# Prompt attention in units of four query tiles, with the values as TensorE's weights in two column halves

## The chip, the cores and the metric

The kernel runs on one NeuronCore of one Trainium2 chip. The metric is the device time of one execution in microseconds (us). TensorE (PE) multiplies matrices: it loads a block of weights and streams another operand past it, into PSUM. VectorE (DVE), ScalarE (ACT) and GpSimd (POOL) work element by element, and SyncE (SP) issues the transfers between HBM and SBUF. Each engine takes its instructions in the order of its own list and waits on semaphores for the others.

## The reference

One decoder layer for two groups: a prompt of 1024 tokens and 8 sample requests of 4 tokens each with 4096 cached tokens in pages. The layer has a mixer (a gated MLP, and attention over latents with 8 heads), attention to a memory, and a gated FFN with a short convolution. The change lies in the mixer. Cut to its core:

```python
def chunk_gmlp(u, v, w_s, b_s, ln_g, ln_b):          # the gate of phase 1
    vg = layer_norm(gelu(v).reshape(n, t // c, c, A_GROUPS, A_GROUP_DIM), ln_g, ln_b)
    mixed = einsum('gts,nmsgd->nmtgd', tril(w_s), vg) + b_s...
    return gelu(u) * mixed.reshape(n, t, A_WIDTH)

q = qk_rope(rms_norm((rms_norm(cq) @ w_uq)...))      # 8 heads, 64 + 32 (rope)
k = qk_rope(rms_norm(concat([ckv_n @ w_uk, k_pe])))
v = ckv_n @ w_uv                                     # 8 heads x 64
s = einsum('...qhd,...khd->...hqk', q, k) * 96 ** -0.5
p = softmax(where(k_pos <= q_pos, s, NEG_INF))
b_out = einsum('...hqk,...khd->...qhd', p, v)
x = x + concat([rms_norm(a_out), rms_norm(b_out)]) @ w_o
```

All inputs and outputs are float32.

## The kernel before

The stages follow each other in the profiled execution: phase 1 with the projections and the gate (to about 208 us), prompt attention (to 427), the sample's paged attention (to 900), output projection and memory attention (to 1187), FFN (to the end). Helpers come back everywhere: `mm3` (L185) does a product of operands that are split into a high and a low part, as three matmuls; `split` writes the high part on ACT (L191 or L195) and the low part on DVE (L192 or L198); `rsqrt_steps` (L222 to L245) takes a root by two Newton steps, 11 DVE operations, or three on DVE and 13 on GpSimd where it is given that engine. Names in the rows are tiles: kTh and kTl are the two parts of the transposed keys of a head, qTh and qTl of its queries, s a bank of scores in PSUM, pr and prs probabilities, pth their transposed copy, o the output, wsum a block of FFN weights.

**Phase 1.** Tokens are in tiles of 128: eight of the prompt, and the ninth holds the sample's 32. `squares(c)` sums the squares of three tiles on ACT and takes their roots (rs_tok) on DVE. The gate runs in two halves of channels; for each group of tiles it takes gelu (ACT L457), a layer norm (DVE L458 to L472), a split (vgh, vgl) and the product with wsh, wsl on TensorE. The order of the four engines is what a scheduler made of the code in this phase.

**Prompt attention** (`phase2a`, L640). Its order is written out by hand, under `manual_schedule`. `proj_group` projects latents to q, k and v for half of the heads (hf) and tiles i0 to i1, and norms them (L855 to L876, rope on GpSimd, L602 to L605); `head_prep` transposes q and k of one head (L899) and splits them. `head_unit` gives the functions of one unit, which is one head and **two query tiles** (G = 0 to 3): scores with the row maximum (L923 to L932; keys in one chunk up to 512, else in two; the s banks are two), `expo` (L936), `trans` (transposes of the probabilities to keys by queries and a copy on ACT, L945 and L947), `value` (L957: pth, 128 keys by 128 queries, is the weight, and 64 columns of v stream by), and `out` (reciprocal of the sum, product into b_all or b_last). 32 units make 80 steps. A step transposes bank j of its unit, writes out what is done, does the exps that are pending, computes scores of the unit **two ahead**, and does the values of the step before. The lists `extra` put the other work into steps: head_prep of the next heads, projections of the second half of the heads, and from step 22 on, every four steps, `weight_sums`, which GpSimd forms for the FFN from 1 MB blocks (13 of them, four operations of 128x512 each, L794 to L797). Three of the four groups of two tiles are normed and transposed for the output projection (`mix_steps`, L1536 to L1552) in the last steps, one in the sample's attention. `sample()` starts the sample's preparation and its first page loads at step 41.

**Start of prompt attention.** Before the first unit, all of q and k of the first four heads is projected and normed, and head 0 is transposed whole. `proj_weights` loads and splits the second heads' weights at that place.

## Time and profile before

| | |
|---|---|
| median of three runs | 1867.06 us (1865.72 to 1868.98) |
| the profiled execution | 1869.48 us |
| its span, first to last instruction | 1867.6 us |
| busy: PE, PE's weight loads, DVE, ACT, POOL | 98%, 94%, 73%, 50%, 36% |
| mean granted clock of TensorE | 0.988 |

The busy shares are averages over stages. A row of a group shows line, engine, operation, output and inputs with their sizes, the count, the busy time and the mean ns of one; behind the second bar stands the idle time ahead of them and what ended it. Matmuls overlap, so that the mean of one is longer than the distance between two starts. The granted clock is 1.00 at full speed. In a row of the timeline the first number is the start in us, the second the time to the end of the group.

### The profile page before, as it was taken

How to read it: one execution, taken by the hardware profiler on the slowest of the kernel's cores; microseconds unless marked ns; L12 is line 12 of the kernel's file. 1: busy time of each engine (PE TensorE's matmuls, PEld its weight loads, DVE VectorE, ACT ScalarE, POOL GpSimd, SP SyncE). 2: the span in 40 equal slices, each digit the busy share in tenths (PEclk: the TensorE clock that was granted, in tenths of full speed). 3: DMA queues.
4: the chain of work that ended last, by engine and by line, in shares of the span. 5: the costliest groups of instructions: out<-in, count | busy, mean ns of one | idle time of the engine just before them, and what ended most of it. 6: DMA issues, size and time to landing. Idle time of an engine off the chain costs nothing.

```text
span 1867.6 us, 39666 instructions
## 1 busy us (share of the span) xinstructions
PE 1823.0 (98%) x14414; PEld 1754.7 (94%) x14414; DVE 1355.3 (73%) x2824; ACT 928.1 (50%) x1965; POOL 679.1 (36%) x784
## 2 busy tenths in 40 slices
PE   9999899989999999999999999999999999999999
PEld 8899899888999999998899988899999999999999
DVE  7864756655877767776744675888888888879664
ACT  7335776665555555555543455533323333344442
POOL 0011306643535445443313110267776677500000
PEclk9999899989999999999999999999999999999999
DMA  8102205556776666564554345412222222495252
GB/s 321 41 10 67 79 1 193 213 214 190 216 207 182 181 172 194 164 187 132 178 167 132 127 159 152 140 59 85 77 90 82 69 79 71 118 349 170 76 154 76
DMA packets 129414, 260.17 MB, mean 139 GB/s; under 512 B 20417, under 2 KB 70434, under 8 KB 126146
## 3 DMA queue, kind: packets, MB, share of 16 engines
q1 hardware_dynamic: 128354, 256.58, 43.7%
q8 instruction: 114, 1.87, 0.4%
q10 hardware_dynamic: 864, 1.05, 0.2%
q14 instruction: 82, 0.67, 0.1%
HBM read 212.27 MB, written 45.30 MB: 138 GB/s over the span
## 4 chain that ended last, share of the span: by engine, by line
PE 81%; issue 5%; DMA 4%; DVE 4%; SPq 3%; ACT 2%; POOL 2%; DVEq 0%; POOLq 0%; ACTq 0%
PE s L185 15%; PE d L185 12%; PE mm L185 9%; PE F L185 7%; PE b L185 7%; PE X L185 7%; PE E L185 7%; PE A L185 3%; PE o L957 3%; PE y L185 3%; PE tp L945 1%; SPq L1248 1%; DMA cT<-cT 1%; PE o L1395 1%; DMA ck<-ck 1%
## 5 line engine op out<-in xcount | busy, mean ns | idle before, releaser
L185 PE MATMUL s<-w2h,ch 128*128 128x288 f32 (+1 forms) x1024 | 303.8, 297 | 0.3 <-DVE S L1319 0.3
L185 PE MATMUL s<-w2h,cl 128*128 128x288 f32 (+1 forms) x1024 | 295.8, 289 | 3.5 <-POOL cl L1280 3.5
L185 PE MATMUL s<-w2l,ch 128*128 128x288 f32 (+1 forms) x1024 | 294.6, 288 | 0.0
L185 PEld LDWEIGHTS s<-w2h,ch 128*128 128x128 f32 x1024 | 192.6, 188 | 8.8 <-issue 2.5
L185 PEld LDWEIGHTS s<-w2h,cl 128*128 128x128 f32 x1024 | 192.4, 188 | 5.3 <-POOL cl L1280 5.3
L185 PEld LDWEIGHTS s<-w2l,ch 128*128 128x128 f32 x1024 | 192.8, 188 | 0.0
L1323 DVE TENSOR_REDUCE ss<-sq 128x16 f32<-128x1024 f32 x128 | 155.2, 1213 | 31.0 <-ACT sq L1320 30.5
L1280 POOL TENSOR_TENSOR cl<-cT,ch 128x512 fp32r<-128x512 f32 x64 | 82.9, 1295 | 119.4 <-ACT ch L1276 107.9
L1320 ACT ACTIVATE sq<-s 128x512 f32<-128x512 f32 x128 | 76.6, 598 | 87.6 <-PE s L185 87.6
L1317 ACT ACTIVATE sq<-s 128x512 f32<-128x512 f32 x128 | 76.8, 600 | 75.8 <-PE s L185 69.7
L191 ACT CAST a<-brb 128x528 fp32r<-128x528 f32 x77 | 48.8, 634 | 110.6 <-PE d L185 107.3
L192 DVE TENSOR_TENSOR a<-brb,a 128x528 fp32r<-128x528 f32 x77 | 54.3, 707 | 57.4 <-ACT a L191 57.2
L185 PE MATMUL d<-a,w 128*128 128x264 f32 x768 | 95.4, 284 | 0.4 <-DVE G L2117 0.4
L185 PEld LDWEIGHTS d<-a,w 128*128 128x128 f32 x768 | 94.3, 188 | 0.6 <-issue 0.6
L957 PEld LDWEIGHTS o<-v,pth 128*128 128x128 f32 x576 | 77.1, 200 | 7.3 <-ACT pth L947 5.1
L957 PE MATMUL o<-v,pth 128*128 128x64 f32 x576 | 77.4, 277 | 4.9 <-ACT pth L947 4.6
L1988 POOL TENSOR_TENSOR lo<-s,hi 128x1024 fp32r<-128x1024 f32 x20 | 62.8, 3141 | 45.7 <-ACT hi L1987 45.7
L185 PE MATMUL mm<-whi,xh 128*128 128x256 f32 (+3 forms) x272 | 78.2, 288 | 0.0
L185 PE MATMUL mm<-wlo,xh 128*128 128x256 f32 (+3 forms) x272 | 77.5, 287 | 0.0
L185 PE MATMUL mm<-whi,xl 128*128 128x256 f32 (+3 forms) x272 | 77.4, 288 | 0.0
L1276 ACT CAST ch<-cT 128x512 fp32r<-128x512 f32 x128 | 73.4, 626 | 5.5 <-DMA cT<-cT 5.5
L2043 ACT COPY a<-A 128x264 f32<-128x264 f32 x43 | 16.1, 375 | 118.7 <-PE A L185 113.9
(738 smaller groups left out, 6425.5 us busy)
## 6 DMA issues: line engine op xcount, KB each, us to landing
cT<-cT SPq DMA_DIRECT2D x256, 160.0 KB, 2.7
ck<-ck SPq DMA_DIRECT2D x256, 144.0 KB, 3.4
raw<-w_up SPq DMA_DIRECT2D x44, 512.0 KB, 3.6
wsumd<-wsum SPq DMA_DIRECT2D x13, 1024.0 KB, 5.1
actd<-cv SPq DMA_DIRECT2D x44, 264.0 KB, 2.6
brb<-actd SPq DMA_DIRECT2D x44, 264.0 KB, 5.7
wsum<-w_down SPq DMA_DIRECT2D x11, 1024.0 KB, 4.9
raw<-wsumd SPq DMA_DIRECT2D x20, 512.0 KB, 3.8
```

The source lines that it names most:

```text
L185: self.nc.tensor.matmul(out, l, r, start=first and i == 0, stop=last and i == len(seq) - 1)
L191: {"act": nc.scalar.copy, "pool": nc.gpsimd.tensor_copy, "dve": nc.vector.tensor_copy}[eng](hi, src)
L192: low = lambda: nc.vector.tensor_tensor(lo, src, hi, ALU.subtract)
L945: nc.tensor.transpose(tp[:, z * P : z * P + P], u[e][:, jj * P : jj * P + P], self.ident)
L957: nc.tensor.matmul(u["o"][:, e], th[:, z * P : z * P + P], s["v"][:, jj, h % 4], start=j == z == 0, stop=e == 1 and jj == 2 * G + 1)
L1248: dmas.append([nc.sync.dma_start(cT[:, j], I["cT"][bass.ds(rv, 1)].rearrange("a p n -> (a p) n")) for j, rv in enumerate(rvs)])
L1276: nc.scalar.copy(d["h"][:, k], src[k])
L1280: (nc.vector if k else nc.gpsimd).tensor_tensor(d["l"][:, k], src[k], d["h"][:, k], ALU.subtract)
L1317: nc.scalar.activation(sq[:, 0], ps[:, :, n0 : n0 + 256], AF.Square)
L1320: nc.scalar.activation(sq[:, 1], pt.rearrange("p (e d) -> p e d", e=2), AF.Square)
L1323: yield lambda: nc.vector.tensor_reduce(s["ss"][:, g0 : g0 + 2].rearrange("p e (z h) -> p z e h", z=2), sq.rearrange("p z e (h d) -> p z e ...
L1988: eng.tensor_tensor(lo, src, hi, ALU.subtract)
```

## The change

- `squares`: the roots of the second and third group of tiles run on GpSimd.
- A unit is one head and **four** query tiles: 16 units. The first of a head (G = 0) has 3 steps, the second (G = 1) has 4, in which two banks each are transposed and multiplied, and one at the end: 56 steps. Scores are computed one unit ahead, at steps given by `places`; where the second unit of a head comes up, its first two tiles (640 and 768 keys) are in one step.
- `value`: v of one head (128 keys by 64) is the weight, and the transposed probabilities of one or two tiles (128 or 256 columns) stream by. Even tiles of the unit go to PSUM partitions 0 to 63, odd ones to 64 to 127. So the output is transposed: `copy` brings it to SBUF two steps after the unit's end, and `out`, a step later, transposes it back in two blocks and multiplies by the reciprocals.
- The first unit uses only q and k of tiles 0 to 3. The norm of tiles 4 to 7 is issued between its scores, the one of the sample's tile in steps 0 to 3, and k and q of the second half are transposed in step 0. The value projections of tiles 4 to 7 stand between the scores. The second heads' weights are loaded early and split in steps 2 and 3.
- `weight_sums` works on halves of 512 KB (26 of them, four operations of 128x256 each), from step 4 on, spread over 45 steps.
- The projections of the second heads are spread over steps 11 to 31. `sample()` starts at step 32 of 56.
- Two groups of two tiles (0 to 3) are mixed in prompt attention, started when heads 0 to 7 of tiles 0 to 3 are written. Tiles 4 and 5 go to DRAM (`b_dram`) after the last unit and are read back ahead of the sample's first page loads; they and tiles 6 and 7 are mixed in the sample's attention.

```diff
@@ squares
-            self.rsqrt(pl, self.rs_tok[:, 3 * c : 3 * c + 3], ss, 1.0 / 1024)
+            for _ in self.rsqrt_steps(pl, self.rs_tok[:, 3 * c : 3 * c + 3], ss, 1.0 / 1024, nc.gpsimd if c else None):
+                pass
...
@@ phase2a
-        for f in qk + v + qk1[:5] + v1[:2] + qk1[5:9] + qk2[:3] + qk1[9:] + v1[2:] + qk2[3:]:
+        (qk, v), (qk1, _), (qk2, _) = gs
+        for f in qk + v + qk1[:9] + qk2[:3]:
             f()
+        norm, norm_s = qk1[9:], qk2[3:]
...
+        order = [(h, G) for h in range(6) for G in range(2)] + [(6, 0), (7, 0), (6, 1), (7, 1)]
...
+        for n in range(1, len(units)):
+            places = {(1, 0): (0, 0, 1, 2), (0, 1): (-1, -1, 0, 1), (0, 0): (0, 0, 1, 1), (1, 1): (0, 1, 1, 2)}
+            at = places[order[n - 1][1], order[n][1]] if n > 1 else (0, 0, 1, 1)
+            for e in range(4):
+                jobs[starts[n - 1] + at[e]].append((units[n], e))
+
+        put(split_w, (2, 2, 3, 3))
+        spread(norm_s, 0, 4)
...
+        sums = [(i, z) for i in (NK, NK + 1, *range(NK)) for z in range(2)]
+        for j, x in enumerate(sums):
+            extra[4 + j * 45 // len(sums)].append(lambda x=x: self.weight_sums(half(), *x))
...
+            for f in preps[0][0], preps[0][1]:
+                f()
+            v1[0]()
+            for e in range(4):
+                units[0]["a"](e)
+                norm[e]()
+                if e:
+                    units[0]["e"](e - 1)
+                    if e % 2:
+                        v1[e // 2 + 1]()
+            units[0]["e"](3)
+            for f in norm[4:]:
+                f()
+            v1[3]()
...
+                for k, banks in enumerate(u["steps"]):
                     self.flush()
+                    for b in banks:
+                        u["T"](b)
+                    for f in outs.pop(t, []):
                         f()
                     for f in pend:
                         f()
+                    if t == 0:
+                        for f in preps[0][2:]:
+                            f()
+                        self.flush()
                     pend = []
+                    for w, e in jobs[t]:
+                        w["a"](e)
+                        pend.append(lambda w=w, e=e: w["e"](e))
                     self.flush()
+                    for f in V:
+                        f()
+                    V = [lambda u=u, b=b: u["V"](b) for b in banks]
+                    if k == len(u["steps"]) - 1:
+                        outs.setdefault(t + 2, []).append(u["copy"])
+                        outs.setdefault(t + 3, []).append(u["out"])
+                        if order[n] == (7, 0):
+                            outs[t + 3].append(lambda: steps.extend((mix(0, "k"), mix(1, "q"))))
...
+        nc.sync.dma_start(self.b_dram, b_all[:, 4:])
...
@@ head_unit
+        J = 4 * G
+        banks = [[(j, e) for e in (0, 2, 1, 3)] for j in range(J + 1)]
+        banks += [[(J + 3, 3), (J + 1, 2), (J + 1, 1), (J + 1, 3)], [(J + 2, 2), (J + 2, 3)]]
+        u = {"steps": [[0, 1], [2, 3], [4, 5], [6]] if G else [[0], [1], [2]]}
...
-                nc.tensor.matmul(
-                    u["o"][:, e], th[:, z * P : z * P + P], s["v"][:, jj, h % 4], start=j == z == 0, stop=e == 1 and jj == 2 * G + 1
+            for j, e, z, m in runs:
+                g, o = e % 2 * 64, e // 2 * P
+                nc.tensor.matmul(
+                    u["o"][g : g + 64, o : o + m * P], s["v"][:, j, h % 4], th[:, z * P : (z + m) * P],
+                    start=j == 0, stop=b == len(banks) - 1,
                 )
+        def copy():
+            u["oc"] = self.t(p, [P, 256], F32, "oc", 2)
+            nc.vector.tensor_copy(u["oc"], u["o"])
+            nc.vector.reciprocal(u["r"], u["r"])
+
         def out():
+            tp = self.t(pp, [P, 512], F32, "tp", 4)
+            for z in range(2):
+                nc.tensor.transpose(tp[:, z * P : z * P + P], u["oc"][:, z * P : z * P + P], self.ident)
+            x = tp[:, :256].rearrange("p (e d) -> p e d", e=4)
+            d = slice(h * 64, h * 64 + 64)
+            for a, z, dst in ((0, 2, self.b_all[:, 4:6]), (2, 4, self.b_last)) if G else ((0, 4, self.b_all[:, :4]),):
+                nc.vector.tensor_tensor(dst[:, :, d], x[:, a:z], u["r"][:, a:z].unsqueeze(2).broadcast_to([P, z - a, 64]), ALU.mult)
...
```

Three places show how the lists of the engines change. The first is ACT's list in the gate of phase 1. rs_tok holds the roots, gv the gelus (the one that reads st_473 before and st_484 now is of tile 6, and the one behind it of tile 7), a_all the other half of the gate, vgh the cast of the normed values. Before:

```order
L191 CAST vgh_396<-gv_399 128x256 x3
L486 ACTIVATE a_all_90<-mm_778,rs_tok_67 128x256
L462 ACTIVATE gsq_548<-gv_527 128x256
L486 ACTIVATE a_all_90<-mm_804,rs_tok_67 128x256
L457 ACTIVATE gv_656<-st_473,rs_tok_67 128x256
L457 ACTIVATE gv_656<-mm_498,rs_tok_67 128x256
L486 ACTIVATE a_all_90<-mm_830,rs_tok_67 128x256
L462 ACTIVATE gsq_663<-gv_656 128x256
```

And now:

```order
L191 CAST vgh_402<-gv_405 128x256 x2
L487 ACTIVATE a_all_91<-mm_789,rs_tok_67 128x256
L191 CAST vgh_402<-gv_405 128x256
L458 ACTIVATE gv_667<-st_484,rs_tok_67 128x256
L458 ACTIVATE gv_667<-mm_509,rs_tok_67 128x256
L487 ACTIVATE a_all_91<-mm_815,rs_tok_67 128x256
L463 ACTIVATE gsq_674<-gv_667 128x256
L463 ACTIVATE gsq_681<-gv_667 128x256
```

The gelus of tiles 6 and 7 stood behind two more a_all after the casts that read gv_399; now they stand behind one.

The second place is TensorE's list at the start of prompt attention. k_2409 and k_2573 are the keys of tiles 0 to 3 and 4 to 7 before, k_2418 is that of tiles 0 to 3 now; the rows with wvh and wvl are value projections of tiles 4 to 7, those with s are scores of the first unit. Before:

```order
L185 MATMUL mm_2752<-wvl_1746,ckh_1690 128x256
L185 MATMUL mm_2752<-wvh_1745,ckl_1691 128x256
L899 MATMUL tp_2797<-ident_60,k_2409 96x128 x4
L899 MATMUL tp_2804<-ident_60,k_2573 96x128 x4
L899 MATMUL tp_2813<-ident_60,q_2410 96x128 x4
L899 MATMUL tp_2822<-ident_60,q_2574 96x128 x4
L185 MATMUL s_2886<-kTh_2795,qTh_2811 128x128
L185 MATMUL s_2886<-kTl_2796,qTh_2811 128x128
L185 MATMUL s_2886<-kTh_2795,qTl_2812 128x128
```

And now (the rows left out repeat the three with wvh and wvl):

```order
L185 MATMUL mm_2692<-w2l_1695,ckh_1701 32x256
L185 MATMUL mm_2692<-w2h_1694,ckl_1702 32x256
L930 MATMUL tp_2727<-ident_60,k_2418 96x128 x4
L930 MATMUL tp_2736<-ident_60,q_2419 96x128 x4
L185 MATMUL tp_2743<-wvh_1748,ckh_1701 128x256
L185 MATMUL tp_2743<-wvl_1749,ckh_1701 128x256
L185 MATMUL tp_2743<-wvh_1748,ckl_1702 128x256
...
L185 MATMUL s_2754<-kTh_2725,qTh_2734 128x128
L185 MATMUL s_2754<-kTl_2726,qTh_2734 128x128
L185 MATMUL s_2754<-kTh_2725,qTl_2735 128x128
L185 MATMUL s_2772<-kTh_2725,qTh_2734 128x256
```

All value projections and four groups of transposes stood ahead of the first scores; now it is two groups and one projection, and the others follow between the scores.

The third is TensorE's list within a unit: transposes of probabilities (L945, now L977), scores of a coming unit (L185), values (L957, now L992), and the transposes of a finished output (L1005). Before:

```order
L185 MATMUL s_5136<-kTh_4965,qTl_5053 128x128
L957 MATMUL o_5142<-v_2829,pth_5080 128x64 x3
L945 MATMUL tp_5146<-ident_60,prs_933_5000 128x128
L945 MATMUL tp_5146<-ident_60,prs_942_5040 128x128 x2
L185 MATMUL s_5157<-kTh_4965,qTh_5052 128x256
L185 MATMUL s_5157<-kTl_4966,qTh_5052 128x256
L185 MATMUL s_5157<-kTh_4965,qTl_5053 128x256
L957 MATMUL o_5163<-v_2829,pth_5124 128x64 x4
L945 MATMUL tp_5175<-ident_60,pr_953_5085 128x128
L945 MATMUL tp_5175<-ident_60,pr_957_5098 128x128
```

And now:

```order
L977 MATMUL tp_3092<-ident_60,pr_441_2931 128x128
L977 MATMUL tp_3092<-ident_60,pr_437_2918 128x128
L977 MATMUL tp_3092<-ident_60,pr_427_2882 128x128
L977 MATMUL tp_3092<-ident_60,pr_441_2931 128x128
L1005 MATMUL tp_3099<-ident_60,oc_3050 128x128 x2
L185 MATMUL s_3106<-kTh_2951,qTh_2981 128x512
L185 MATMUL s_3106<-kTl_2952,qTh_2981 128x512
L185 MATMUL s_3106<-kTh_2951,qTl_2982 128x512
L992 MATMUL o_3063<-pth_3037,v_2405 64x256 x2
L992 MATMUL o_3063<-pth_3044,v_2405 64x256 x2
L977 MATMUL tp_3124<-ident_60,pr_437_2918 128x128
L977 MATMUL tp_3124<-ident_60,pr_441_2931 128x128
```

A bank's values were four matmuls of 64 columns with pth as weights; they are two of 256 columns (or one and two of 128) with v as weights, two banks to a step, and the output's own transposes have come in.

## The prediction

> **What bounds the kernel now.** I read the page first, then the stretches by window, the waits of TensorE, and last the timeline around each wait.

> ```profile
> span 1867.6 us, 39666 instructions
> PE 1823.0 (98%) x14414; PEld 1754.7 (94%) x14414; DVE 1355.3 (73%) x2824; ACT 928.1 (50%) x1965; POOL 679.1 (36%) x784
> PEclk9999899989999999999999999999999999999999
> ```

> TensorE is busy 98% of the span; the other engines have room on average. So a change pays only where it takes work from TensorE or closes one of its few gaps. The clock dips in the second, fifth and ninth slices show where gaps lie. The sum below is made against the profiled execution: 1869.5 us (span 1867.6), 2.4 above the median of the runs, 1867.06.

> Next come TensorE's waits, in phase 1 and then in prompt attention.

> ```profile
> PE mm L185 <- ACT vgh L191: 4.1, 1, 4.1
> ...
> PE tp L899 <- DVE rqh L235: 5.9, 1, 5.9
> PE s L185 <- DVE pr L930: 4.6, 8, 2.1
> PE o L957 <- ACT pth L947: 4.6, 1, 4.6
> PE s L1295 <- DVE k L1549: 1.0, 1, 1.0
> ```

> The next rows are the stretches right behind the four longest waits (us, then busy time and count of PE, PEld, DVE, ACT and POOL, then the granted clock).

> ```profile
> 66.30:72.30 6.00, 6.00 (x25) 5.61 (x26) 4.57 (x18) 0.00 (x0) 0.00 (x0) 0.52 0.55 181
> 214.40:222.40 8.00, 7.90 (x29) 6.75 (x30) 6.28 (x23) 4.03 (x9) 1.45 (x4) 0.51 0.01 2
> 304.30:311.30 7.00, 6.96 (x31) 6.93 (x32) 3.23 (x11) 1.02 (x3) 5.06 (x5) 0.52 0.70 286
> 413.40:423.80 10.40, 10.38 (x51) 10.39 (x52) 4.84 (x24) 5.65 (x12) 0.00 (x0) 0.51 0.14 52
> ```

> A wait costs more than its length: TensorE then works for 6 to 10 us at half clock. Busy time times (1 - clock) is what that loses: 2.9, 3.9, 3.3 and 5.1 us. Wait and clock together: 7.0 at the gate of phase 1, 9.8 at the start of attention, 2.1 + 3.3 = 5.4 in its middle, 9.7 at its end, and 3.5 in small waits (1.0, and 4.6 - 2.1). So 35 us is all that better covered waits can give.

> **Values.** This is the one edit that takes matmul work away.

> ```profile
> L957 PE MATMUL o<-v,pth 128*128 128x64 f32 x576 | 77.4, 277 | 4.9 <-ACT pth L947 4.6
> 370.26 1.00 PE L957 MATMUL o<-v,pth 128*128 128x64 f32 x8
> 371.10 0.60 PE L899 MATMUL tp<-ident,k 128*96 128x128 f32 x4
> 371.54 0.49 PE L945 MATMUL tp<-ident,pr 128*128 128x128 f32 x3
> ```

> The busy time of a group overlaps its neighbours, so I price by starts: eight instructions in 371.10 - 370.26 = 0.84, or 0.105 each, though each streams only 64 columns; four transposes of 128 columns take 371.54 - 371.10 = 0.44, 0.11 each. A value instruction thus costs no less than one of 128 columns. I take 0.11 for both: 576 x 0.11 = 63.4 us.

> After, a value matmul has V (64 columns) as weights and streams 128 or 256 probabilities into one half of the output's partitions, two instructions each as before. 288 blocks of 128 x 128 at two instructions are the same columns; the gain depends on whether the two column halves run at once. The profile has such a case in the sample's attention: four 32-column strips, matmuls of 257 columns.

> ```profile
> 527.25 0.28 PE L185 MATMUL s<-w2l,ch 128*128 128x256 f32 x1
> 527.37 0.28 PE L185 MATMUL s<-w2h,cl 128*128 128x256 f32 x1
> 527.58 1.07 PE L1395 MATMUL o<-ck,S 128*32 128x257 f32 x16
> 528.58 0.40 PE L185 MATMUL s<-w2h,ch 128*128 128x288 f32 x1
> 528.82 0.29 PE L185 MATMUL s<-w2l,ch 128*128 128x288 f32 x1
> ...
> 527.58 0.42 PE L1395 MATMUL o<-ck,S 128*32 128x257 f32 x4
> ...
> 528.25 0.40 PE L1395 MATMUL o<-ck,S 128*32 128x257 f32 x4
> ```

> The first five rows are the whole stretch; the last two are what narrow windows near its start and its end hold: four instructions at a time. 16 instructions in four rounds take 528.58 - 527.58 = 1.00. Three rounds lie between 527.58 and 528.25: 0.22 each, so 0.11 per 128 columns here too. In turn the 16 would take 3.5. A matmul of 256 columns ahead of it starts 0.12 after the one before. So entering costs (527.58 - 527.37) - 0.12 = 0.09, the stretch 1.00 - 0.88 = 0.12 over its rounds, and the first matmul behind it 0.24 to its successor's start where 288 columns need 0.14: together 0.31 per stretch.

> The longer half of each step decides. In units of 128 columns, a unit of the first four tiles has 2 + 3 + 1 = 6, one of the second four 4 + 4 + 5 + 1 = 14 (the fifth step holds a bank with three blocks in one half): 20 per head, 8 x 20 x 2 x 0.11 = 35.2 us. One stretch in each of 56 steps adds 56 x 0.31 = 17.4. Together 52.6 against 63.4: -10.8. Bounds: entry free, -28; halves in turn, 63.4 + 17.4, +17. I take -10.8 because the strips are the nearest row.

> **Output.** o now comes out transposed. Per unit DVE copies it (128x256) and TensorE transposes two blocks: 32 x 0.11 = +3.5 us on the path. On DVE, 32 products and 32 reciprocals become 16 copies, 16 reciprocals and 24 products: no more than before, and DVE has room there (22.6 busy of 30 us in a window quoted below). Copy and transposes stand two and three steps behind the unit's end, so neither is waited for: 0.

> **The roots in phase 1.** The 4.1-us wait has its cause on DVE, 15 us earlier.

> ```profile
> 50.59 0.16 DVE L236 SCALAR_TENSOR_TENSOR rs_tok<-rqh,rqy 128x3 f32<-128x3 f32 x1
> 47.59 0.47 ACT L486 ACTIVATE a_all<-mm,rs_tok 128x256 f32<-128x256 f32 x1 [0.99 <-PE mm L185]
> 51.23 0.47 ACT L457 ACTIVATE gv<-st,rs_tok 128x256 f32<-128x256 f32 x1
> 66.27 1.22 PE L185 MATMUL mm<-vgh,wsh 128*128 128x512 f32 x2 [4.10 <-ACT vgh L191]
> ...
> L588 POOL CAST cksl<-ckl 128x32 fp32r<-128x32 f32 x2 | 0.4, 208 | 0.0
> ```

> The root of the last tokens takes its turns in DVE's queue until 50.75; the gate of tiles 6 and 7 follows: gelu at 51.23, norm and cast, matmul at 66.27. On GpSimd, idle then, 13 operations replace 8 of DVE's: at the 0.21 of its smallest ones, 2.7 us. In ACT's new order this gelu stands behind the a_all of 47.59 and one cast, so it can start at about 48.4, 2.8 us earlier, and 16 instructions in all leave DVE, which carries the rest of the chain. About 3 of the 4.1 us go, and with so short a wait half of the 2.9 of clock: -4.5. Bounds: 0, if DVE's queue gives nothing back, and -7.0.

> **First unit on half the tokens.** Before, the four transposes of k (second half) waited for the norm of tiles 4 to 7.

> ```profile
> 207.94 0.60 PE L899 MATMUL tp<-ident,k 128*96 128x128 f32 x4
> 214.40 1.09 PE L899 MATMUL tp<-ident,k 128*96 128x128 f32 x4 [5.86 <-DVE rqh L235]
> 197.56 0.18 DVE L863 TENSOR_TENSOR rq<-hr,sq_tok 128x16 f32<-128x16 f32 x1
> 208.50 0.54 DVE L192 TENSOR_TENSOR wql<-pth,wqh 128x384 fp32r<-128x384 f32 x1
> ```

> The first half's norm was done at 197.7, ten us before use. After, only k0 and q0 are transposed first; the value projections (24 matmuls of 256 columns at 0.12, 2.9 us) and the scores of tiles 0 to 3 fill in while the second norm runs, without the weight splits (wql at 208.50) in DVE's queue. What is late next: unit 0's own chain. Its first scores wait for the splits of k0 and q0 (ACT's half and then 0.7 on DVE, some 2 us in all, less 0.7 of projection), its first transposes for four exps in a row. I take 3 us of waiting left and half of the clock loss, 5 of 9.8: -4.5. Bounds 0 and -9.8.

> **Middle.** The wait at 302.3 follows a queue on GpSimd.

> ```profile
> 281.57 1.30 POOL L794 TENSOR_TENSOR wsum<-wsum 128x512 f32<-128x512 f32 x1
> 298.68 1.05 POOL L876 TENSOR_TENSOR k<-kr,hr 128x512 f32<-128x512 f32 x1 [0.65 <-DVE rsum L962]
> 303.20 0.69 DVE L192 TENSOR_TENSOR kTl<-tp,kTh 96x512 fp32r<-96x512 f32 x1 [1.44 <-ACT kTh L191]
> ```

> Eight weight sums from 281.57 to 293.1 stood ahead of the rope and of k, and so of kTl. Halves of 256 columns, begun at step 4 of 56, put four operations of half that width, some 2.6 us, ahead of it at a time, and begin long before the rope comes. What is late next may be the rope itself, whose projections now share ACT with earlier exps. -3.5; bounds -5.4 and +3.

> **End.** At 408.8 the value matmuls waited 4.6 us for pth, whose copy stood on ACT behind an exp, itself 2.37 us late, and behind squares of the mixes.

> ```profile
> 408.97 1.24 ACT L936 ACTIVATE pr<-pr,nm,rq 128x1024 f32<-128x1024 f32 x1 [2.37 <-DVE nm L932]
> 411.43 0.61 ACT L1536 ACTIVATE q<-b_all 128x512 f32<-128x512 f32 x1
> ```

> Two mixes instead of three now run in prompt attention, and they start six steps before its end, so they still meet the last exps. -4; bounds -9.7 and +2.

> **New waits.** Scores run one unit ahead, not two, with the same two score buffers, and each exp stands one step before its transposes. Where the second unit of a head begins, two rows of tiles (640 and 768 columns) come in one step: four chunks through two buffers.

> ```profile
> L930 DVE TENSOR_SCALAR_CACHE_REDUCE pr<-s 128x320 f32<-128x320 f32 (+3 forms) x32 | 18.8, 586 | 7.2 <-PE s L185 6.8 <-ACT pth L947 0.2
> 270.00:300.00 30.00, 29.11 (x223) 27.94 (x222) 22.58 (x75) 22.00 (x84) 20.11 (x22) 1.00 0.26 81
> ```

> DVE takes 0.59 on average per chunk, TensorE about 0.5 (three matmuls of 320 to 384 columns at 0.12 per 256), so a chunk or two is waited for, 0.5 us, eight times; for an exp about 0.3, eight times; and where the second heads' projections load ACT (22.0 of 30 us before, last row), 2. Sum +8; bounds 0 and +20 (eight waits of 1.5, some losing clock). This is my least known term.

> **Sample.** The tiles 4 and 5 of the output go out to DRAM and come back on SP ahead of the first pages, and their mix runs within the sample's attention.

> ```profile
> ck<-ck SPq DMA_DIRECT2D x8, 144.0 KB, 6.2
> ```

> The store waits for the last product, and SP's page loads wait behind it. The pages land 6.2 us after issue, and the first sample scores had other work ahead of them: +1.5, bounds 0 and +4. Eight transposes move from one stretch to the other: 0.

> **Sum.** -10.8 + 3.5 - 4.5 - 4.5 - 3.5 - 4 + 8 + 1.5 = -14.3: 1869.5 becomes 1855.2, and the median 1867.06 becomes 1853.

> **Rivals.**
> - The waits nearly vanish, or entering the halves costs little (-12 from either): 1841. For it: the waits' causes are named and moved. Against: ACT and DVE get less lead.
> - The terms of waiting come out at half their gain (+8): 1861. For it: DVE and ACT keep nearly the same work, so that the next link can be late; against: the causes named are single ones.
> - The second half starts a round behind the first, since each half's two instructions stand together in the queue: 56 x 0.22 = 12, 1865. Against it: four starts at 527.58, with two instructions per strip there too. [...]
> - The lead is too short, and this decides alone: the first double step of each second unit holds TensorE as the one DVE wait of 2.1 us did, at 2.1 + 3.3 with its clock. Eight times 5.4 is 43 instead of the 4 counted there: 1853 + 39 = 1892. It turns slower from 2.3 us lost at each (8 x 2.3 less the 4 is the whole gain). Against it: before, too, wide chunks went through two buffers, and eight waits made only 4.6 in all.
> - The halves don't run at once: 1853 + 28 = 1881. The strips speak against it, but they are a quarter of the array, not half.

> **How the numbers follow.** The sum 0.48 (own range 1845 to 1861); the good rival 0.15; half gains 0.16; a round behind 0.06; short lead 0.10; halves in turn 0.05. A difference under 0.2%, 3.7 us, can't be told from no change: a time from 1863.3 to 1870.8. Of half gains a quarter lies there, of a round behind two thirds; the last two are slower. Faster 0.48 + 0.15 + 0.12 + 0.02 = 0.77; same 0.08; slower 0.15. The range 1835 to 1870 leaves out the two slow cases (0.15) and the far end of the good one (0.04).

> **What would show it.** In the values' rows, 352 instructions with 64-column outputs, starting in pairs, about 1 us from the first of a two-bank step to the work behind it; a start 0.2 later for the second half would mean strict order, all in turn serial halves. No wait above 2 us at 62, 208 and 302. DVE waits of scores at the beginnings of the second units, each below 1 us; exps directly ahead of their transposes. It is wrong if the clock falls below 0.9 between 225 and 400, or if the first page's scores wait more than 4 us.

## The result, and the profile after

The changed kernel takes 1878.1 us (median of seven runs, 1875.3 to 1881.1) against 1868.1 for the kernel before in the same series. The ratio is 1.0049, with an interval from 1.0031 to 1.0066: about 9 us slower, where I had forecast 14 us less. Run again later beside two other kernels it came out at 1.0066 (1.0049 to 1.0083). All runs below but the two with four edits had the kernel before beside them and not the changed kernel, so they are set against both of these ratios. Of the kernel before with its weight sums in halves, one execution of six took 2933.7 us at a granted clock of 0.554, and the figures given for it are those of the other five. The page of the profile:

```profile
span 1877.4 us, 39366 instructions
PE 1820.9 (97%) x14222; PEld 1713.6 (91%) x14222; DVE 1351.9 (72%) x2800; ACT 927.3 (49%) x1965; POOL 700.4 (37%) x862
```

TensorE is busy 2 us less than before in a span that is 10 us longer: it did not get more work, it waits more. TensorE's waits, in phase 1 and then in prompt attention:

```profile
PE mm L185 <- ACT vgh L191: 3.6, 1, 3.6
...
PE s L185 <- DVE qTl L198: 5.4, 5, 2.0
PE tp L977 <- ACT cn L1045: 5.4, 1, 5.4
PE tp L977 <- ACT pr L969: 5.1, 4, 2.4
PE s L185 <- DVE pr L964: 2.0, 6, 0.9
PE s L185 <- ACT qTh L195: 1.9, 3, 0.8
```

The long waits of before (5.9 at the start, 2.1 in the middle, 4.6 at the end) are gone, and the waits for scores at DVE, which I feared, are 2.0 us. But there are waits for qTl and qTh, for exps (pr), and one of 5.4 us for cn, a tile of the sample's preparation. Prompt attention as a whole, before and after, then the stretches behind five of the waits (us, busy time and count of PE, PEld, DVE, ACT, POOL, then the granted clock):

```profile
207.90:428.60 220.70, 205.01 (x1501) 192.04 (x1499) 143.56 (x504) 148.78 (x402) 89.05 (x91) 0.93 0.38 139
```

```profile
203.00:432.20 229.20, 204.13 (x1325) 151.44 (x1323) 140.43 (x488) 146.42 (x411) 96.37 (x142) 0.93 0.43 137
215.00:227.00 12.00, 10.73 (x44) 8.04 (x42) 8.67 (x34) 3.74 (x8) 0.00 (x0) 0.72 0.00 1
353.00:365.00 12.00, 8.85 (x39) 6.65 (x40) 3.31 (x12) 6.17 (x19) 8.45 (x16) 0.59 0.66 218
329.00:335.00 6.00, 6.00 (x34) 4.33 (x34) 2.50 (x10) 2.26 (x5) 0.00 (x0) 0.74 0.27 87
389.00:395.00 6.00, 5.85 (x30) 3.91 (x29) 3.83 (x18) 2.84 (x9) 2.01 (x4) 0.72 0.91 290
419.00:425.00 6.00, 4.70 (x26) 3.15 (x27) 2.70 (x16) 5.58 (x11) 0.00 (x0) 0.72 0.00 0
```

TensorE idles 25.1 us in the stage, where it idled 15.7, and the stage is 8.5 us longer, 2.9 us of value projections included that stood ahead of it before. Busy time times (1 - clock) behind the waits is 3.0, 3.6, 1.6, 1.6 and 1.3 us. Outside the stage, its start comes 4.9 us earlier (203.0 for 207.9), and what follows it takes 1445.2 us where it took 1439.0.

The 5.4 us have a chain of four rows on three engines:

```profile
350.12 0.72 POOL L822 TENSOR_TENSOR wsum<-wsum 128x256 f32<-128x256 f32 x1 [6.15 <-DMA wsum<-w_down]
355.39 0.30 POOL L1044 MEMSET cn<- 128x258 f32 x1
355.73 0.36 ACT L1045 COPY cn<-tp 32x256 f32<-32x256 f32 x1 [8.16 <-POOL cn L1044]
356.15 0.69 PE L977 MATMUL tp<-ident,pr 128*128 128x128 f32 x2 [5.37 <-ACT cn L1045]
```

GpSimd waited 6.15 us for the load of a half of the weight sums; the memset of cn stood behind it in its list, behind the half's four operations and 2.2 us of other memsets and a copy for the sample; ACT's copy into cn waited 8.16 us for that, with copies of pth and an exp behind it. TensorE's transposes began at 356.15, 0.06 us after ACT's copy had ended. That copy empties one of the four tp buffers, and the transposes write into such a buffer; so it is the buffer that they seem to have waited for.

### The profile page after: what moved, and what is told of

Its sections match the earlier page's. It is cut to its first block, busy times and chain, and to the rows that moved or that the text cites. A ratio compares the mean times of both kernels' runs of the same rounds, so it can differ in the third digit from the quotient of the medians.

```text
span 1877.4 us, 39366 instructions
## 1 busy us (share of the span) xinstructions
PE 1820.9 (97%) x14222; PEld 1713.6 (91%) x14222; DVE 1351.9 (72%) x2800; ACT 927.3 (49%) x1965; POOL 700.4 (37%) x862
## 3 DMA queue, kind: packets, MB, share of 16 engines
q10 hardware_dynamic: 864, 1.05, 0.2%
## 4 chain that ended last, share of the span: by engine, by line
PE 78%; issue 6%; DVE 4%; DMA 4%; SPq 3%; POOL 2%; ACT 2%; POOLq 0%; DVEq 0%; ACTq 0%
PE s L185 13%; PE d L185 12%; PE mm L185 9%; PE b L185 8%; PE F L185 7%; PE X L185 7%; PE E L185 7%; PE A L185 3%; PE y L185 3%; PE o L992 2%; DMA cT<-cT 2%; PE tp L977 1%; SPq L1297 1%; SPq L1301 1%; PE tp L185 1%
## 5 line engine op out<-in xcount | busy, mean ns | idle before, releaser
L185 PE MATMUL s<-w2h,ch 128*128 128x288 f32 (+1 forms) x1024 | 305.1, 298 | 0.0
L185 PE MATMUL s<-w2h,cl 128*128 128x288 f32 (+1 forms) x1024 | 297.4, 290 | 4.2 <-POOL cl L1329 4.2
L185 PE MATMUL s<-w2l,ch 128*128 128x288 f32 (+1 forms) x1024 | 296.0, 289 | 0.0
L185 PEld LDWEIGHTS s<-w2h,ch 128*128 128x128 f32 x1024 | 194.0, 189 | 8.3 <-issue 2.5
L185 PEld LDWEIGHTS s<-w2h,cl 128*128 128x128 f32 x1024 | 193.8, 189 | 6.3 <-POOL cl L1329 6.3
L185 PEld LDWEIGHTS s<-w2l,ch 128*128 128x128 f32 x1024 | 194.3, 190 | 0.0
L1372 DVE TENSOR_REDUCE ss<-sq 128x16 f32<-128x1024 f32 x128 | 155.3, 1214 | 32.1 <-ACT sq L1369 31.6
L191 ACT CAST a<-brb 128x528 fp32r<-128x528 f32 x77 | 48.8, 634 | 112.8 <-PE d L185 108.7
L185 PE MATMUL d<-a,w 128*128 128x264 f32 x768 | 95.4, 284 | 1.0 <-DVE G L2166 1.0
L185 PEld LDWEIGHTS d<-a,w 128*128 128x128 f32 x768 | 94.3, 188 | 1.2 <-issue 1.2
L192 DVE TENSOR_TENSOR a<-brb,a 128x528 fp32r<-128x528 f32 x77 | 54.4, 707 | 56.3 <-ACT a L191 56.3
L185 PE MATMUL mm<-whi,xh 128*128 128x256 f32 (+3 forms) x272 | 77.9, 288 | 0.0
L185 PE MATMUL mm<-wlo,xh 128*128 128x256 f32 (+3 forms) x272 | 77.5, 287 | 0.0
L185 PE MATMUL mm<-whi,xl 128*128 128x256 f32 (+3 forms) x272 | 77.4, 288 | 0.0
L185 PE MATMUL d<-a,hi 128*128 128x264 f32 x552 | 72.0, 284 | 0.0
L2155 POOL TENSOR_TENSOR cv<-cv,row 128x1056 f32<-128x1056 f32 x22 | 63.5, 2887 | 19.1 <-ACT cv L2154 19.1
## 6 DMA issues: line engine op xcount, KB each, us to landing
ck<-ck SPq DMA_DIRECT2D x256, 144.0 KB, 3.4
```

Source lines behind the costliest of these rows:

```text
L185: self.nc.tensor.matmul(out, l, r, start=first and i == 0, stop=last and i == len(seq) - 1)
L191: {"act": nc.scalar.copy, "pool": nc.gpsimd.tensor_copy, "dve": nc.vector.tensor_copy}[eng](hi, src)
L192: low = lambda: nc.vector.tensor_tensor(lo, src, hi, ALU.subtract)
L1372: yield lambda: nc.vector.tensor_reduce(s["ss"][:, g0 : g0 + 2].rearrange("p e (z h) -> p z e h", z=2), sq.rearrange("p z e (h d) -> p z e ...
L2155: nc.gpsimd.tensor_tensor(cv, cv, row, ALU.mult)
```

## The experiments

### The sample's preparation off GpSimd

```diff
-        nc.gpsimd.memset(self.cn, 0.0)
+        nc.vector.memset(self.cn, 0.0)
...
```

The same is done to the copy of qr and the memsets of bd and bdq.

> The changed kernel, with the copies and memsets of the sample's preparation (qr, bd, bdq, cn) on DVE instead of GpSimd. Theory A (GpSimd's list): in the changed kernel ACT's copy cn waited 8.2 us for a memset that stood on GpSimd behind a weight sum, which itself waited 6.2 us for its load; TensorE's transposes waited 5.4 us behind that and then ran at half clock (3.3 us lost). Off GpSimd, the 5.4-us wait goes and no other takes its place: 8 to 9 us less than the changed kernel's 1878, about 1869.5. Rival B (the lead of the exps is too short, so that ACT is late there anyhow): a wait of 2 us or more stays at that place, and the time falls by less than 4 us.

Measured: 1869.2 us, 1.0022 of the kernel before (1.0009 to 1.0035). The 5.4 us wait is gone and TensorE waits only 0.4 us for cn:

```profile
PE tp L1005 <- ACT cn L1045: 0.4, 1, 0.4
```

Against the changed kernel's 1.0049 to 1.0066 that is 5 to 8 us. Theory A holds, a little below its size; rival B falls.

### Three buffers for the weight sums

```diff
-        half = lambda: self.t(pm, [P, 2, 2, 256], F32, "wsum", 2)
+        half = lambda: self.t(pm, [P, 2, 2, 256], F32, "wsum", 3)
...
-            th = u["t", b] = self.t(p, [P, 512], F32, "pth", 6)
+            th = u["t", b] = self.t(p, [P, 512], F32, "pth", 5)
```

> The changed kernel, with three buffers for the halves of the weight sums instead of two (and five instead of six for pth, to make room). Theory A: a half needs its load (3.6 us), four operations (2.9) and its store (3.4), so two buffers give one half per 5 us, and GpSimd waits for loads 67 us in all, with rope, keys and memsets queued behind; three buffers cut these waits below 25 us, the 5.4-us wait of TensorE goes with its clock, and rope and keys come earlier: 9 to 11 us less, 1867 to 1869. Rival C (the transfers themselves are slow, since they compete with each other): GpSimd's waits stay above 50 us and the time stays within 3 us of 1878.

Measured: 1869.7 us, 1.0021 (1.0008 to 1.0033). GpSimd's waits for these loads in prompt attention, first the changed kernel, then this one:

```profile
POOL wsum L822 <- DMA wsum<-w_down: 53.0, 15, 16.0
...
POOL wsum L822 <- DMA wsum<-w_up: 14.3, 2, 8.0
```

```profile
POOL wsum L822 <- DMA wsum<-w_down: 17.4, 9, 2.9
```

67 us of waiting became 17 (with one wait of 6.3 us beside them for which the profile names no releaser), and the wait for cn went with it. So the transfers are not slow: two buffers kept them from running ahead. Rival C falls. The gain is 5 to 8 us, not the 9 to 11 of theory A, and the waits for q, exps and the first unit stayed.

### The weight sums in halves, alone, in the kernel before

```diff
-            wsums = dict(zip(range(22, 75, 4), (NK, NK + 1, *range(NK))))
+            wsums = dict(zip(range(22, 74, 2), [(i, z) for i in (NK, NK + 1, *range(NK)) for z in range(2)]))
...
```

With it goes the changed kernel's `weight_sums` on halves of 512 KB.

> The kernel before, with one part of the change alone: the weight sums in 26 halves of 512 KB, every two steps from step 22, in place of 13 blocks every four. My prediction gave shorter pieces a gain of 3.5 us (the 2.1-us wait of TensorE in the middle and the half clock behind it). Theory J: a half costs its load, its operations and its store with nearly the same latencies as a whole block, two buffers give one half per 5 us and no faster, GpSimd's waits for loads rise from 33 us to over 50, and the time stays within 3 us of the kernel before or rises by up to 5. Rival: the wait in the middle goes and nothing comes in its place, 3 to 5 us less.

Measured: 1877.6 us (median of five, 1875.4 to 1894.0) against 1865.5 for the kernel before, 12 us more; the ratio is 1.0092 (1.006 to 1.0124). That is no less than the whole change costs. GpSimd's waits for loads before and in this run:

```profile
POOL wsum L794 <- DMA wsum<-w_down: 33.2, 8, 17.6
```

```profile
POOL wsum L795 <- DMA wsum<-w_down: 51.9, 17, 15.6
...
POOL wsum L795 <- DMA wsum<-w_up: 5.5, 1, 5.5
```

And the rows in which it reaches TensorE:

```profile
342.28 0.36 ACT L1003 COPY cn<-tp 32x256 f32<-32x256 f32 x1 [6.97 <-POOL cn L1002]
343.16 1.54 PE L958 MATMUL o<-v,pth 128*128 128x64 f32 x6 [4.73 <-ACT pth L948]
```

It is the same chain as in the changed kernel as far as ACT; here TensorE's values wait for the pth copy behind the copy of cn. The 2.1-us wait in the middle, which my prediction had expected to go, is still there. Theory J has the mechanism and understates the price: the waits for loads rise to 57 us, the 4.7-us wait is new, and the time rises by 12 us in the medians where it allowed 5. The profiled execution of this run, at 1875.4 us, is its fastest one and shows some 6 us of that. A load of 512 KB landed in 3.6 us in the changed kernel where one of 1 MB took 4.9 in the kernel before (medians of the two pages), so half the bytes did not take half the time.

### q and k a step earlier

```diff
-            put(preps[h], {3: (9, 10, 11, 13), 4: (22, 23, 25, 26), 6: (36, 37, 39, 40), 7: (40, 41, 44, 46)}.get(h, (b + 1, b + 2, b + 2, b + 4)))
+            put(preps[h], {3: (9, 9, 11, 13), 4: (22, 22, 25, 25), 6: (36, 36, 39, 39), 7: (40, 40, 44, 45)}.get(h, (b + 1, b + 1, b + 2, b + 3)))
```

> The changed kernel, with the transposes and splits of the next head's q and k one step earlier where they stood one step ahead of their first scores. Theory D: TensorE waits 7.3 us in all for qTl and qTh (five and three times, up to 2.0), and after two of these waits it loses 1.6 us each to the half clock; a step more takes these waits below 2 us in all: 7 to 9 us less than 1878, about 1870. Rival (ACT is the bound in these steps): the waits turn up at the next transposes of probabilities, and the time stays within 3 us of 1878.

Measured: 1871.4 us, 1.0036 (1.002 to 1.0051): 2 to 6 us less, with an interval that overlaps the changed kernel's. What stood there, in the changed kernel:

```profile
325.67 0.73 DVE L198 SCALAR_TENSOR_TENSOR qTl<-tp,ggq,qTh 96x512 fp32r<-96x512 f32 x1
326.45 0.41 PE L185 MATMUL s<-kTh,qTl 96*128 96x320 f32 x1 [1.98 <-DVE qTl L198]
```

The q of a head was transposed at 322.5, split by ACT at 323.2 to 323.9, and DVE came to its low part at 325.7, behind ten small operations of a norm. A step earlier the waits for qTl are gone, those for qTh are 1.2 us. The waits for cn stand at 6.6 us (5.4 and 4.7 in the two traces of the changed kernel), those for scores at DVE at 3.9 (2.0 and 3.4). About half of theory D's gain.

### The old start

All norms, the value projections and the whole of head 0 ahead of the first unit again, in the changed kernel:

```diff
+            for f in v1[:2] + norm + v1[2:] + norm_s + preps[0]:
+                f()
...
-                    if t == 0:
-                        for f in preps[0][2:]:
-                            f()
-                        self.flush()
```

> The changed kernel with one part undone: all norms and value projections, and all four transposes of head 0, ahead of the first unit as before. My prediction gave the new order 4.5 us; the trace of the changed kernel shows seven short waits of 4.7 us in all between 203 and 216 and half clock behind them. Theory E (the one long wait became many short ones with the same loss of clock, so the part is worth nothing): within 2 us of 1878. Rival (it is worth what I gave it): 4 to 6 us more, 1882 to 1884.

Measured: 1879.4 us, 1.0075 (1.0049 to 1.0101), beside 1.0049 and 1.0066 for the changed kernel: 1.7 to 5 us more. In the traces the stretch from the last projection to the first score of the second head is 28.7 us in the changed kernel (202.9 to 231.6) and 31.8 here (202.5 to 234.3). The two stretches:

```profile
202.90:231.60 28.70, 22.02 (x120) 16.59 (x117) 19.23 (x74) 16.53 (x56) 2.87 (x6) 0.88 0.00 1
```

```profile
202.50:234.30 31.80, 23.68 (x119) 18.22 (x116) 20.02 (x71) 16.92 (x56) 3.99 (x7) 0.79 0.00 1
```

Busy time times (1 - clock) is 2.6 and 5.0 us, so most of the 3.1 us is half clock: it lasted 6.8 us there in the changed kernel and 13.7 here. The new start itself took 28.4 to 29.0 us in all other traces but the one of the run with four edits, where half clock lasted 17.1 us and the stretch 31.6. One trace of the old start can't tell the order's own worth from that spread, and ratios with overlapping intervals can't either: theory E and my 4.5 are both left open.

### The mixes a step later

```diff
-                            outs[t + 3].append(lambda: steps.extend((mix(0, "k"), mix(1, "q"))))
+                            outs.setdefault(t + 4, []).append(lambda: steps.extend((mix(0, "k"), mix(1, "q"))))
```

> The changed kernel, with the two mixes of prompt attention started one step later, behind the last exp instead of ahead of it. Theory F: near the end ACT did four squares of the mixes (2.7 us) ahead of the last exp of 1024 columns, TensorE's transposes waited 2.45 us for it, and half clock followed (1.3 us lost before the sample's attention and some 2 behind its start). Without it 3 to 5 us less than the changed kernel. Rival (the mixes are as late as they are early: what they lose at the end they win here): the mixes' own transposes then come last, a wait of 1 us or more stands ahead of the sample's first scores, and the time stays within 2 us.

Measured: 1874.6 us, 1.0062 (1.0046 to 1.0078); the changed kernel measured in the next series was at 1.0066. In the changed kernel ACT had the squares ahead of the last exp:

```profile
415.91 0.62 ACT L1585 ACTIVATE k<-b_all 128x512 f32<-128x512 f32 x1
...
418.91 1.24 ACT L969 ACTIVATE pr<-pr,nm,rq 128x1024 f32<-128x1024 f32 x1
```

In this run the 2.45-us wait is gone (2.6 us for exps are left, 1.3 at most), and 1.0 us for pth and 1.5 us ahead of the last two transposes of the output are there instead. A single edit that moves 2 us cannot be told from none by these times.

### The values as the moving operand again

The changed kernel, with its units and steps, but probabilities as weights, v in 64 columns behind them, and the output not transposed:

```diff
+                nc.tensor.matmul(
+                    u["o"][:, e * 64 : e * 64 + 64], th[:, z * P : z * P + P], s["v"][:, j, h % 4],
...
```

> The changed kernel with one part undone: the values as the moving operand again (64 columns, probabilities as weights, 576 instructions), the output not transposed, units and steps as changed. Theory G (the form is worth what its rows cost): in the traces the old form takes 0.615 us for six instructions and 0.84 for eight, 60 us in all; the new one 51.5 us with its entries, and the output's transposes 3.5; so undoing it costs 60 - 55 = 5 us: 4 to 6 us more than the changed kernel. Rival H (in these units ACT and DVE set the pace, and what TensorE saves it waits): within 2 us of the changed kernel, with 3 to 6 us less of waits. My prediction's own price would make it 7 more.

Measured: 1879.1 us, 1.0065 (1.0046 to 1.0084), the same as the changed kernel. So the time does not show what the form saves; the last experiment sets the rows beside each other.

### The roots on DVE again

```diff
-            for _ in self.rsqrt_steps(pl, self.rs_tok[:, 3 * c : 3 * c + 3], ss, 1.0 / 1024, nc.gpsimd if c else None):
+            for _ in self.rsqrt_steps(pl, self.rs_tok[:, 3 * c : 3 * c + 3], ss, 1.0 / 1024, None):
```

> The changed kernel with one part undone: all roots of phase 1 on DVE again. Theory I: on GpSimd the last group's roots took 7.6 us instead of 2.7 (single operations of 1.1 to 2.1 us where DVE works at the same time, 0.2 where it doesn't), after a mask that itself waited 4.0 us for TensorE, and rs_tok came at 51.1 as on DVE before; the part is worth at most 2 us: 0 to 2 us more than the changed kernel, the first matmul of the gate at 65 to 67 us. Rival (it is worth my 4.5): 4 to 5 more.

Measured: 1876.2 us, 1.0063 (1.0048 to 1.0078), not slower. The wait at the gate is 4.1 us with DVE and 3.6 with GpSimd:

```profile
PE mm L185 <- ACT vgh L191: 4.1, 1, 4.1
```

Theory I holds, with the rows of the changed kernel behind it:

```profile
41.02 2.37 POOL L406 TENSOR_SCALAR_AFFINE_SELECT ws<-ws 128x1024 f32<-128x1024 f32 x1 [4.03 <-PE mm L185]
43.50 2.10 POOL L238 TENSOR_TENSOR rqa<-rqy 128x3 f32<-128x3 f32 x1
50.88 0.20 POOL L245 TENSOR_TENSOR rs_tok<-rqh,rqy 128x3 f32<-128x3 f32 x1
51.12 0.48 ACT L458 ACTIVATE gv<-st,rs_tok 128x256 f32<-128x256 f32 x1 [3.14 <-POOL rs_tok L245]
```

The roots stood behind a mask that waited 4.0 us for TensorE, then took 7.6 us, and the gelu came at 51.1 as before.

### Three edits together, and a fourth

> The changed kernel with three buffers for the weight sums, the earlier q and k, and the later mixes together. If the three causes are apart, their gains add: 4.5 + 2.5 + 3.5, some 10 us less than the changed kernel, within 3 us of the kernel before. Rival (each frees the next wait at the same place, above all ACT's exps): 5 to 7 less.

Measured, with three buffers, the earlier q and k and the later mixes: 1863.4 us, 0.9991 (0.9982 to 1.0001). The gains add: 11 to 14 us less than the changed kernel. A new wait stood in the trace, on DVE's list this time:

```profile
385.05 0.75 DVE L1113 TENSOR_SCALAR cosT<-cosT,cols 128x1024 f32<-128x1024 f32 x1 [4.75 <-DMA cosT<-c_cosT]
386.99 0.50 PE L185 MATMUL s<-kTh,qTh 96*128 96x512 f32 x1 [3.21 <-DVE pr L964]
```

The sample's cosines are scaled for a later stage, and their load was late; DVE waited, and TensorE's scores behind it. So the fourth edit delays that scaling by six steps:

```diff
-        yield
+        for _ in range(6):
+            yield
         nc.vector.tensor_scalar(self.cosT, self.cosT, self.col("gk_rep"), None, ALU.mult)
```

The changed kernel was run beside it:

> The changed kernel as it is, beside the next two on the same chip, as their measure. In the theory that chips differ little: 1.004 to 1.007 of the kernel before, with the 5-us wait ahead of cn and the waits for qTl in the same places; a rival would be a ratio below 1.003, by which the gains of the single runs would be differences of chips.

> Three buffers for the weight sums, the earlier q and k, the later mixes, and the scaling of the sample's cosines six steps later: in the last run with the first three, a wait of 3.2 us stood where DVE's list had that scaling, which waited 4.8 us for its load. If these in-order waits are what separates the changed kernel from its matmul work, the 3.2 and some 2 us of half clock go: 5 us less than with three changes, 0.996 to 0.998 of the kernel before. Rival: the clock's losses behind (5 us in the sample's attention in that run) and the first pages' loads take it back: 0.999 or more.

Measured: 1878.7 us, 1.0066 (1.0049 to 1.0083) for the changed kernel, with waits of 4.7 us for cn and 5.3 for qTl as in its first trace, and 1859.6 us, 0.9966 (0.9951 to 0.9981) with the four edits. The 3.2-us wait is gone (0.9 at most). That is 19 us less than the changed kernel and faster than the kernel before by 0.3%.

### The form of the values, with few other waits

> The run before with the values as the moving operand again and no transposes of the output: the form of the values alone, among few other waits. Theory G: the rows (62 us of old matmuls in these units, 51.5 of new ones with their entries, 3.5 of transposes) make it 6 to 8 us slower than the run before. Rival H (other engines set the pace of these steps): within 2 us of it.

Measured: 1861.9 us, 0.9981 (0.9969 to 0.9992), 2.3 us more than with the new form, between the two theories; the two intervals overlap, so that the times alone hardly tell the two forms apart. Prompt attention to the sample's first scores, new form and then old:

```profile
201.90:415.40 213.50, 199.52 (x1328) 147.95 (x1325) 137.78 (x490) 147.09 (x413) 97.07 (x143) 0.96 0.47 146
```

```profile
203.70:419.90 216.20, 202.76 (x1517) 187.97 (x1516) 130.79 (x470) 146.90 (x413) 98.00 (x144) 0.98 0.45 143
```

Busy time at the granted clock, 199.52 x 0.96 = 191.5 and 202.76 x 0.98 = 198.7, differs by some 7 us (the clocks are printed to two digits, which is worth 1 us each): theory G is right about the work. The stage is only 2.7 us shorter, since the new form ran longer at half clock (8.0 against 4.1 us). The first 33 us of the stage, again new form and then old:

```profile
201.90:234.90 33.00, 27.43 (x131) 20.59 (x129) 20.61 (x74) 17.82 (x57) 4.31 (x8) 0.74 0.04 10
```

```profile
203.70:236.70 33.00, 25.38 (x155) 21.04 (x153) 23.23 (x83) 20.41 (x64) 5.99 (x10) 0.90 0.03 9
```

TensorE waits in the same places there in both, 1.3 us at the longest, but the clock was 0.74 against 0.90. The form doesn't bring it: in the other eight traces with the new form and the new start half clock lasted 6.8 us before 226, as in both traces with the old form; only this one has 17.1. Since one execution is profiled of each run, what the others did with the 7 us of work, of which the medians show 2.3, stays open.

## Why the prediction was wrong, point by point

The sum was wrong by 24 us (-14.3 forecast, +9.8 between the two profiled executions). Step by step:

- **What a wait costs** held on the whole: behind most longer waits TensorE ran at half clock for some us. How long was luck, as far as these runs show. The same wait of 3.6 us at the gate was followed by 3.4 us of half clock in the changed kernel's first trace, by 6.8 in its second and by none in the run with four edits:

```profile
60.00:75.00 15.00, 11.43 (x73) 10.58 (x71) 12.49 (x36) 3.99 (x9) 0.00 (x0) 0.89 0.21 72
```

```profile
60.00:75.00 15.00, 11.43 (x62) 10.30 (x60) 11.37 (x35) 4.42 (x8) 0.00 (x0) 0.77 0.22 72
```

```profile
60.00:75.00 15.00, 11.43 (x86) 10.53 (x84) 12.81 (x38) 4.73 (x9) 0.00 (x0) 1.00 0.23 74
```

- **Values**: the mechanism was right, the two halves run at once. In the changed kernel:

```profile
302.56 0.44 PE L992 MATMUL o<-pth,v 128*64 128x128 f32 x4
302.93 0.66 PE L977 MATMUL tp<-ident,pr 128*128 128x128 f32 x4
...
304.92 0.65 PE L992 MATMUL o<-pth,v 128*64 128x256 f32 x4
305.50 0.64 PE L930 MATMUL tp<-ident,k 128*96 128x128 f32 x4
```

  Four instructions of 128 columns, two per half, take 0.37 us, of 256 columns 0.58: two rounds and 0.15. Of the first four, two begin at 302.56 to 302.57 and two at 302.72 to 302.73. So the rivals "a round behind" and "in turn" fall. 56 stretches came to 43.0 us, and with 0.15 on the matmuls around each of them to 51.5, where I had 52.6. The old form was over-priced: 63.4, where its stretches add up to 60.0. Net -8.5 instead of -10.8, by rows; the time of the changed kernel shows none of it.
- **Output**: +3.5 for the transposes held; TensorE waited for a copy only at the last unit, 0.5 us.
- **Roots**: -4.5 was wrong: the wait fell from 4.1 to 3.6. The clock's loss behind it fell from 2.9 to 1.7 in the first trace, but by the rows above that is the execution's and not the roots'. The step that failed is "at the 0.21 of its smallest ones, 2.7 us" on an "idle" GpSimd: its list had the mask, which waits for TensorE, and its operations took up to 2.1 us.
- **First unit**: 3 us by the undone part, most of it half clock, where I had 4.5; what the order alone is worth stays open. What is late next was named rightly (unit 0's own chain): seven waits of 4.7 us in all by 216, and 3.0 us of half clock behind them.
- **Middle**: here the sign was wrong. I wrote that halves "put four operations of half that width, some 2.6 us, ahead of it at a time" and gave that -3.5. I counted the operations and not the load that each group waits for. GpSimd's waits for loads rose from 33 to 67 us, and each of them is a wait for everything behind it in its list; with a third buffer they were 17. Alone, this part costs the kernel before 12 us in the medians (11 to 23 by the ratio's interval). This is the step that failed: a gain of 3.5 where the runs show a loss.
- **End**: 9.7 us became 2.45 and 1.3 of clock up to 425: better than my -4, though the clock's share of both is one execution's.
- **New waits**: +8 with bounds 0 and +20 was the right place for the miss and had the wrong reasons. The double chunks cost 2.0 us in all (3.4 in the second trace), where I had put 4 and built the rival "short lead" on them. The second step that failed stands here: what came instead is named nowhere in the prediction, 5.4 + 3.6 us for cn, and 7.3 us for qTl and qTh with 3.2 us of clock. I priced the lead of the scores and exps, but not that of q and k, nor what else stands in ACT's list.
- **Sample**: the +1.5 wasn't needed: the first scores waited 0.7 us, and for GpSimd, not for a page. The sample's attention was 3 to 4 us longer in the profiled execution, which lost 5 us there to half clock where the kernel before lost 1.6. The second trace of the changed kernel lost 2.9, and the runs with edits between 0 and 5, so it isn't laid to the change. In the memory attention behind it TensorE waited 2.2 us for a load (skT; 1.5 in the second trace, no such wait before); no run says whether that is the change's.

The measured time lies above the range's upper end, 1870. The sum of the bounds I had written would have reached past 1880, but I gave the two slow cases 0.15, and neither of them is what happened. Of the signs I named, the wait at 62 stayed (3.6 us, not under 2), the scores' waits at DVE were below 1 us each as hoped (1.8 at most in the second trace), and the clock between 225 and 400 was 0.94, so that the sign of being wrong that I had set at 0.9 didn't show.

## What to carry to other kernels

Before a stream of loads is cut into smaller pieces, count what its consumer's list will wait per piece, not what a piece computes: with two buffers, 8 waits of 33 us in all became 18 of 57 in the kernel before, though the bytes were the same. Memsets and copies that another stage needs should not stand in a list behind an operation that waits for a transfer (the copy of cn waited 8.16 us here). When units grow, every operand's lead has to be counted again, q and k as well as scores (7.3 us of waits for qTl and qTh here).
